# Keeping the rotated queries and keys of retention heads 1 to 3 as two fp32r parts, and loading the parts as operands

## The chip, the core and the metric

The kernel runs on one core of one Trainium2 chip. The metric is the device time of one execution in microseconds (us), shown as the median of several runs. The engines are TensorE (PE, with its weight loads as PEld), VectorE (DVE), ScalarE (ACT), GpSimd (POOL) and SyncE (SP), whose queue issues nearly all DMA transfers.

## What is computed

A trunk of two layers on a sequence of 1024 tokens of width 1024, all in float32. Layer 0 mixes tokens by forgetting attention, layer 1 by retention; each mixer is followed by a SwiGLU feed-forward block of width 2816, all with RMS norms and residuals. The part that matters here is the retention mixer:

```python
q = rotate(q, cos, sin)                 # 4 heads, 256 wide each
k = rotate(k, cos, sin) * (dk ** -0.5)
def rotate(t, cos, sin):
    t1, t2 = t[..., :half], t[..., half:]
    return concatenate([t1 * cos - t2 * sin, t1 * sin + t2 * cos])
# per head, in chunks of 64, with decay:
a = (q @ k.T) * d_intra
inner, cross = a @ v, (q @ state) * q_decay
state = state * chunk_decay + (k * k_decay).T @ v
y = inner + cross    # then normalised over the 512 columns of a head, gated, projected
```

## The kernel before, in words

Activations lie transposed: 128 features on the partitions, 1024 tokens along the row, in two halves of 512 (`HALF`). TensorE multiplies in fp32r. To keep float32 accuracy each operand is held as two fp32r parts, `hi` (the value cast to fp32r) and `lo` (what the cast left over). `split` (L97 to L99) makes them: ScalarE casts (L98), VectorE subtracts (L99). A product of two split operands is three matmuls (hi hi, hi lo, lo hi). The projections use a fast matrix scheme with seven products instead of eight for a 2x2 block of blocks (`Products`, L634 to L676); each product is 4 x 3 matmuls of 512 columns (L653 to L655), and ScalarE copies a sum from one PSUM bank to another or to SBUF between them (L662, L686, L689).

The retention layer has two stages.

*Projections.* `in_turn` (L678) walks over the weight blocks of keys, gates and queries of the four heads, two per head of gates and one each of keys and queries, and hands each result, four 128x512 blocks c11 to c22, to `projected` (L1000). For keys and queries `rotated` (L960 to L971) does the rotation in two halves: four products by cosine and sine on VectorE (L964 to L967), one subtraction and one addition on GpSimd (L968, L969), and two stores of 256 KB through SP into DRAM tiles `qd` or `kd` (L970, L971). In between, `values` (L973) projects the values of each head with `pair_N` (matmuls L771 to L773 of 256 columns) and stores them in `vd`.

*Heads.* `prepare` (L1090) loads a head. `load_k` (L1045) brings the two 128x1024 key tiles of a head into staging tiles `st` (L1050, 512 KB each), splits them into eight operand tiles `b` of pool `bpa` (L1051, through `bsplit` and L98, L99), transposes the same staged data with TensorE (L1060), and scales and splits the transposes (L1065, L1066). `load_units` (L801, called on L1092) loads the two query tiles into `st` (L805) and splits them into eight operand tiles of `bpa`. `load_v` (L1036) loads eight 256 KB blocks of values into `st` (L1038), takes off the mean and splits them into pool `bpb` (L1041 on ScalarE, L1042 on VectorE). Then `scores` (L1105 to L1107, evicted on L1116 and L1121), `weighted` (L1131 to L1133), `crossed` (L1142 to L1144), `state` (L1080 to L1082) and `finish` (L1146) follow for each of the eight pairs of head and half. `prepare(h + 1)` stands in the program at the second half of head h.

Three sets of buffers matter. The staging tag `st` has five tiles of 128x1024 and serves keys, queries, values and weights. `bpa` has 32 operand tiles of 128x512; a head takes 24 of them (8 keys, 4 transposed keys, 8 queries, 4 state). The pool `yp` has 16 tiles tagged `y`, from which `rotated` takes its intermediates.

No order is written out by hand around the change. The program is traced by a framework (the context on L1300) that plans each engine's order of instructions on a timeline of its own before the kernel runs, and places the semaphores. On the chip every engine and the SP queue work strictly in that order, so an instruction that waits holds up everything behind it on its queue.

Of the kernel before, what the change touches and what calls it, by code (L numbers as in the profile page):

```python
# [10 lines left out]
F32 = mybir.dt.float32  # L11
F32R = mybir.dt.float32r
# [5 lines left out]
P = 128  # L18
S = 1024
D = 1024  # L20
KT = D // P
H = 512
# [3 lines left out]
RET_HEADS = 4  # L26
# [11 lines left out]
def trunk(ctx, tc, nc, d, out):  # L38
    cp = ctx.enter_context(tc.tile_pool(name="cp", bufs=1))
    yp = ctx.enter_context(tc.tile_pool(name="yp", bufs=16))  # L40
    dp = ctx.enter_context(tc.tile_pool(name="dp", bufs=1, space=DRAM))

    def const(name, shape):
        t = cp.tile(shape, F32, tag=name, name=name)
        nc.sync.dma_start(t, d[name])
        return t
# [8 lines left out]
    def nm(s):  # L55
        cnt[0] += 1
        return f"{s}_{cnt[0]}"
# [5 lines left out]
    bpa = ctx.enter_context(tc.tile_pool(name="bpa", bufs=32))  # L63
# [4 lines left out]
    def mm_ps():  # L68
        tag, n = (("mm", 3), ("st", 2), ("pv", 2), ("mm", 3), ("st", 2), ("pv", 2), ("mm", 3))[banks[0] % 7]
        banks[0] += 1  # L70
        return mp.tile([P, H], F32, tag=tag, name=nm("mm"), bufs=n)

    def yu(s):
        return yp.tile([P, H], F32, tag="y", name=nm(s))

    def units(pool):
        return [pool.tile([P, H], F32R, tag="b", name=nm("b")) for _ in range(2)]
# [19 lines left out]
    def split(hi, lo, src):  # L97
        nc.scalar.copy(hi, src)  # L98
        return nc.vector.tensor_tensor(lo, src, hi.bitcast(F32), op=ALU.subtract)  # L99
# [10 lines left out]
    HALF = (slice(0, H), slice(H, S))  # L110
# [76 lines left out]
    with ExitStack() as fs:  # L187
# [6 lines left out]
        def half(tag, bufs=2):  # L194
            if tag in ("t", "x"):
                return yp.tile([P, H], F32, tag="y", name=nm(tag))
            return fp.tile([P, H], F32, tag=tag, name=nm(tag), bufs={"rec": 1}.get(tag, bufs))
# [4 lines left out]
        for kt in range(KT):  # L202
            xs = []
            for h in range(2):
                t = half("t", 9)
# [16 lines left out]
        def k_head(h):  # L222
            kh = fp.tile([P, S], F32R, tag="kh", name=nm("kh"))
            kl = fp.tile([P, S], F32R, tag="kl", name=nm("kl"))
            proj_head(2 * h + 1, lambda b, ps: split(kh[:, HALF[b]], kl[:, HALF[b]], ps))
            return kh, kl

        def q_head(h):
            qh = fp.tile([P, S], F32R, tag="qh", name=nm("qh"))
            ql = fp.tile([P, S], F32R, tag="ql", name=nm("ql"))  # L230

            def evac(b, ps):
                t = half("qf")
                nc.vector.tensor_tensor(t, ps, R[:, HALF[b]], op=ALU.mult)
                split(qh[:, HALF[b]], ql[:, HALF[b]], t)

            proj_head(2 * h, evac)
            return qh, ql
# [180 lines left out]
        ks, pss = [], {}  # L419
        for h in range(2):  # L420
            ks.append([fp.tile([P, S], F32R, tag=t, name=nm(t)) for t in ("kh", "kl")])
            for b in range(2):
                tag, n = (("mm", 3), ("mm", 3), ("st", 2), ("st", 2))[2 * h + b]
# [9 lines left out]
        ident = const("ident", [P, P])  # L433
# [12 lines left out]
        qq = q_head(0)  # L446
        for h in range(FOX_HEADS):
            if h > 0:
                kk, qq = k1 if h == 1 else k_head(h), q_head(h)
# [16 lines left out]
        part = {}  # L466
        for i, (n, b) in enumerate(TILES):
            if i < 3:
                mm_u(ops[n, b], wo[n][6:], last_o[:1], b, first=False, last=(i < EVAC))
            else:  # L470
                if n == len(wo):
                    wo.append(wtile(d["fox_o"][n][:, :7 * P], 7))
                tag, bufs = TAGS[i]
# [19 lines left out]
    def bsplit(pool, src):  # L493
        hi, lo = units(pool)
        split(hi, lo, src)
        return hi, lo
# [304 lines left out]
    def load_units(pool, src, gate=None):  # L801

        r = []
        st = sp.tile([P, 1024], F32, tag="st", name=nm("st"), bufs=5)
        nc.sync.dma_start(st, src)  # L805
        if gate is not None:
            gt = sp.tile([P, 1024], F32, tag="st", name=nm("st"), bufs=5)
            nc.sync.dma_start(gt, gate)
            nc.vector.tensor_tensor(st, st, gt, op=ALU.mult)  # L809
        for h in range(2):  # L810
            r.append(bsplit(pool, st[:, HALF[h]]))
        return r
# [102 lines left out]
    for n in range(KT):  # L915
# [3 lines left out]
        for b in range(2):  # L919
            if (n, b) in ops:  # L920
                ps = ops[n, b]
            elif n < NPART:
                ps = mp.tile([P, H], F32, tag=("pv", "st")[b], name=nm("mm"), bufs=2)
            else:
                ps = mm_ps()
# [20 lines left out]
    X, nrm, nw = ffn(0, X, norm, xd, xd2, False, nw, MAP1)  # L946


    qd = [[dp.tile([P, S], F32, tag=f"qd{k}", name=f"qd{k}") for k in range(2 * h, 2 * h + 2)] for h in range(RET_HEADS)]
    kd = [[dp.tile([P, S], F32, tag=f"kd{k}", name=f"kd{k}") for k in range(2 * h, 2 * h + 2)] for h in range(RET_HEADS)]  # L950
    vd = [dp.tile([P, 2 * D], F32, tag=f"vd{k}", name=f"vd{k}") for k in range(TB)]
    gd = [dp.tile([P, S], F32, tag=f"gd{k}", name=f"gd{k}") for k in range(16)]
    zd = [dp.tile([P, S], F32, tag=f"zd{k}", name=f"zd{k}") for k in range(16)]
# [3 lines left out]
        nc.sync.dma_start(cos[h], d["ret_cos"][:, HALF[h]])  # L957
        nc.sync.dma_start(sin[h], d["ret_sin"][:, HALF[h]])

    def rotated(dst, c11, c12, c21, c22):  # L960
        for h, (t1, t2) in enumerate(((c11, c21), (c12, c22))):
            m1, m2, m3 = yu("m1"), yu("m2"), yu("m3")
            m4 = t2 if h else yu("m4")
            nc.vector.tensor_tensor(m1, t1, cos[h], op=ALU.mult)  # L964
            nc.vector.tensor_tensor(m2, t1, sin[h], op=ALU.mult)
            nc.vector.tensor_tensor(m3, t2, sin[h], op=ALU.mult)
            nc.vector.tensor_tensor(m4, t2, cos[h], op=ALU.mult)  # L967
            nc.gpsimd.tensor_tensor(m1, m1, m3, op=ALU.subtract)  # L968
            nc.gpsimd.tensor_tensor(m2, m2, m4, op=ALU.add)  # L969
            nc.sync.dma_start(dst[0][:, HALF[h]], m1)  # L970
            nc.sync.dma_start(dst[1][:, HALF[h]], m2)  # L971

    def values(h):  # L973
        cc = pair_N((d["ret_v"][2 * h], d["ret_v"][2 * h + 1]), X)
# [15 lines left out]
    def gates(p, c11, c12, c21, c22):  # L990
        if p == 0:
            rcs.append(rms(nrm, mp, "ms"))
        for k, h, c in ((0, 0, c11), (0, 1, c12), (1, 0, c21), (1, 1, c22)):
            o = c if h else yu("o")
            nc.vector.tensor_tensor(o, c, R[:, HALF[h]], op=ALU.mult)
            nc.scalar.activation(o, o, AF.Silu)
            nc.sync.dma_start(gd[2 * p + k][:, HALF[h]], o)

    rcs, vmean = [], {}
    def projected(i, *cc):  # L1000
        if i % 4 == 0:
            rotated(kd[i // 4], *cc)
        elif i % 4 == 2:
            rotated(qd[i // 4], *cc)
        else:
            gates(i // 2, *cc)

# [7 lines left out]
    for h in range(RET_HEADS):  # L1015
        srcs = todo[done:4 * h + 3]
        in_turn(srcs, X, lambda i, *cc: projected(done + i, *cc))
        done = 4 * h + 3
        values(h)
    in_turn(todo[done:], X, lambda i, *cc: projected(done + i, *cc))  # L1020

    rc = rcs[0]
# [13 lines left out]
    def load_v(h, b):  # L1036
        st = sp.tile([P, 1024], F32, tag="st", name=nm("st"), bufs=5)[:, :512]
        nc.sync.dma_start(st, vd[b][:, h * 512:(h + 1) * 512])  # L1038
        m = vmean[h][:, b:b + 1]
        hi, lo = units(bpb)  # L1040
        nc.scalar.activation(hi, st, AF.Identity, bias=m)  # L1041
        nc.vector.scalar_tensor_tensor(lo, st, m, hi.bitcast(F32), op0=ALU.add, op1=ALU.subtract)  # L1042
        return hi, lo

    def load_k(h):  # L1045

        ks, kf = [], []
        for e in range(2):
            st = sp.tile([P, 1024], F32, tag="st", name=nm("st"), bufs=5)
            nc.sync.dma_start(st, kd[h][e])  # L1050
            ks.append([bsplit(bpa, st[:, HALF[i]]) for i in range(2)])  # L1051
            kf.append(st)
        kt = []
        for i in range(2):
            ps = mm_ps()
            for b in range(2):
                for e in range(2):
                    tk = slice((2 * i + b) * P, (2 * i + b + 1) * P)
                    c = (2 * b + e) * P
                    nc.tensor.transpose(ps[:, c:c + P], kf[e][:, tk], ident)  # L1060
            hi, lo = units(bpa)
            for b in range(2):
                r = kap[:, h, 2 * i + b:2 * i + b + 1]
                c = slice(b * 256, (b + 1) * 256)
                nc.scalar.activation(hi[:, c], ps[:, c], AF.Copy, scale=r)  # L1065
                nc.vector.scalar_tensor_tensor(lo[:, c], ps[:, c], r, hi[:, c].bitcast(F32),  # L1066
                                               op0=ALU.mult, op1=ALU.subtract)
            kt += [(hi[:, b * 256:(b + 1) * 256], lo[:, b * 256:(b + 1) * 256]) for b in range(2)]
        return ks, kt
# [19 lines left out]

    def prepare(h):  # L1090
        kk, kt = load_k(h)
        qq = [load_units(bpa, qd[h][e]) for e in range(2)]  # L1092
        vv = [load_v(h, b) for b in range(TB)]
        heads[h] = [kk, kt, qq, vv, None, []]

# [50 lines left out]
    def finish(h, ib, yps):  # L1146
# [21 lines left out]
        for vt in range(4):  # L1168
# [5 lines left out]
            nc.sync.dma_start(zd[4 * h + vt][:, HALF[ib]], ys[vt])  # L1174

    prepare(0)
    heads[0][4] = state(heads[0][1], heads[0][3])
    stages = [(h, ib) for h in range(RET_HEADS) for ib in range(2)]
# [21 lines left out]
    for n in range(KT):  # L1200
        w = wtile2(d["ret_o"][n], 8)
        for h in range(2):
            ps = mm_ps()
# [101 lines left out]
```

## Time and profile before

| what | value |
|---|---|
| median of 3 runs | 2585.12 us (2584.18 to 2586.54) |
| profiled execution, own time | 2588.21 us |
| span of its instructions | 2586.4 us |
| granted clock of TensorE over the span | 0.998 |
| moved by DMA over the span | 312.12 MB, mean 121 GB/s |
| projections of the retention layer | about 1140 to 1585 us |
| heads of the retention layer | about 1585 to 1745 us |

The span runs from the first to the last instruction; the profiled execution's own time is 1.8 us longer. A matmul's busy time overlaps the next one's, because matmuls are pipelined, so an engine's busy share is read together with its waits and with the spacing of its instructions. Waits are inferred from semaphores: "A <- B" means that A's engine stood idle and that B ended the wait. Transfers are timed from their issue on the queue to their landing.

### The profile page before, as it was taken

What the parts mean: (1) busy time and instruction counts of PE and PEld (TensorE: products, weight loads), DVE (VectorE), ACT (ScalarE), POOL (GpSimd) and SP (SyncE); (2) the same over time, 40 slices, a digit from 0 to 9 for tenths busy, and PEclk for the clock granted to TensorE, in tenths of its full rate; (3) what the DMA queues carried; (4) which work ended last, traced back from release to release, by engine and by line L of the source; (5) the groups of instructions that cost most, each with busy time, mean ns of one, the idle gap of its engine ahead of it and who ended that gap; (6) DMA issues with size and microseconds to landing.
All of it is one profiled execution on the core that took longest, in us unless ns stands there. A gap on an engine that the chain in (4) does not pass through costs nothing.

```text
span 2586.4 us, 35236 instructions
## 1 busy us (share of the span) xinstructions
PE 2561.6 (99%) x12812; PEld 2183.4 (84%) x12812; DVE 1837.3 (71%) x3130; ACT 1230.9 (48%) x2322; POOL 203.0 (8%) x203
## 2 busy tenths in 40 slices
PE   9999999999999999999999999999999999999998
PEld 8889887888888887889898989898888888888888
DVE  6798888866666767886656576785567666667794
ACT  6566666543333455454343435662354333335543
POOL 0143323000000001001000010000000000000200
PEclk9999999999999999999999999999999999999999
DMA  3111142422332344533232325555522333325541
GB/s 132 44 58 62 54 147 91 154 103 97 114 106 94 124 161 151 185 112 115 102 118 99 110 98 168 187 187 191 204 98 82 110 98 106 103 89 188 168 149 66
DMA packets 138286, 312.12 MB, mean 121 GB/s; under 512 B 16128, under 2 KB 29440, under 8 KB 138112
## 3 DMA queue, kind: packets, MB, share of 16 engines
q1 hardware_dynamic: 132912, 294.65, 33.8%
q0 software_dynamic: 4480, 14.68, 1.7%
q8 instruction: 100, 1.64, 0.3%
q14 instruction: 74, 0.61, 0.1%
q10 hardware_dynamic: 720, 0.55, 0.1%
HBM read 217.54 MB, written 92.27 MB: 120 GB/s over the span
## 4 chain that ended last, share of the span: by engine, by line
PE 92%; DVE 2%; issue 2%; DMA 2%; ACT 1%; POOL 0%; SPq 0%; POOLq 0%; DVEq 0%; ACTq 0%
PE mm L654 18%; PE mm L653 18%; PE mm L655 18%; PE mm L106 7%; PE mm L107 7%; PE mm L108 7%; PE mm L773 2%; PE mm L771 2%; PE mm L772 2%; DMA st<-vd 1%; PE mm L260 1%; PE mm L259 1%; PE mm L258 1%; PE rw L167 1%; PE pv L365 1%
## 5 line engine op out<-in xcount | busy, mean ns | idle before, releaser
L654 PE MATMUL mm<-b,wh 128*128 128x512 f32 x2128 | 827.9, 389 | 1.2 <-DVE b L99 1.2
L653 PE MATMUL mm<-b,wh 128*128 128x512 f32 x2128 | 825.5, 390 | 2.4 <-ACT u L686 1.2
L655 PE MATMUL mm<-b,wl 128*128 128x512 f32 x2128 | 824.4, 389 | 0.0
L98 ACT CAST wh<-st 128x512 fp32r<-128x512 f32 (+4 forms) x450 | 277.2, 617 | 527.5 <-PE mm L654 323.3
L653 PEld LDWEIGHTS mm<-b,wh 128*128 128x128 f32 x2128 | 399.6, 188 | 85.8 <-ACT u L686 1.7
L654 PEld LDWEIGHTS mm<-b,wh 128*128 128x128 f32 x2128 | 399.6, 188 | 83.5 <-DVE b L99 1.6
L655 PEld LDWEIGHTS mm<-b,wl 128*128 128x128 f32 x2128 | 399.5, 188 | 82.8
L99 DVE TENSOR_TENSOR wl<-st,wh 128x512 fp32r<-128x512 f32 (+4 forms) x450 | 318.9, 712 | 190.8 <-ACT wh L98 185.4
L98 ACT CAST wh<-s 128x512 fp32r<-128x512 f32 x252 | 156.9, 624 | 318.0 <-PE mm L654 282.7
L106 PE MATMUL mm<-b,wh 128*128 128x512 f32 x736 | 286.0, 392 | 7.2 <-ACT b L126 5.0
L107 PE MATMUL mm<-b,wh 128*128 128x512 f32 x736 | 287.6, 391 | 1.7 <-DVE b L99 1.7
L108 PE MATMUL mm<-b,wl 128*128 128x512 f32 x736 | 287.2, 391 | 0.0
L99 DVE TENSOR_TENSOR wl<-s,wh 128x512 fp32r<-128x512 f32 x252 | 180.5, 718 | 97.3 <-ACT wh L98 93.2
L106 PEld LDWEIGHTS mm<-b,wh 128*128 128x128 f32 x736 | 138.7, 188 | 36.6 <-ACT b L126 5.4
L107 PEld LDWEIGHTS mm<-b,wh 128*128 128x128 f32 x736 | 138.8, 189 | 29.5 <-DVE b L99 2.2
L108 PEld LDWEIGHTS mm<-b,wl 128*128 128x128 f32 x736 | 138.8, 189 | 28.3
L772 PE MATMUL mm<-wl,b 128*128 128x256 f32 x448 | 126.6, 283 | 0.0
L771 PE MATMUL mm<-wh,b 128*128 128x256 f32 x448 | 126.2, 283 | 0.0
L773 PE MATMUL mm<-wh,b 128*128 128x256 f32 x448 | 126.2, 283 | 0.0
L501 POOL DMA_DIRECT2D b<-ac_B x24 | 13.5, 561 | 1403.8 <-PE mm L654 1400.3
L98 ACT CAST b<-st 128x512 fp32r<-128x512 f32 (+1 forms) x160 | 92.2, 610 | 56.6 <-DVE st L809 18.2
L99 DVE TENSOR_TENSOR b<-st,b 128x512 fp32r<-128x512 f32 (+1 forms) x160 | 103.7, 678 | 13.5 <-ACT b L98 13.3
(507 smaller groups left out, 4047.1 us busy)
## 6 DMA issues: line engine op xcount, KB each, us to landing
st<-ffn_in SPq DMA_DIRECT2D x88, 512.0 KB, 3.5
st<-ffn_out_pairs SPq DMA_DIRECT2D x32, 512.0 KB, 4.0
ac_T<-t SPq DMA_DIRECT2D x48, 256.0 KB, 2.4
xo<-xd SPq DMA_DIRECT2D x32, 256.0 KB, 2.9
ac_B<-t SPq DMA_DIRECT2D x32, 256.0 KB, 2.4
st<-ac_T SPq DMA_DIRECT2D x16, 512.0 KB, 4.8
b<-ac_T POOLq DMA_DIRECT2D x32, 256.0 KB, 5.3
st<-ret_qk SPq DMA_DIRECT2D x16, 512.0 KB, 4.5
```

What stands on the lines that cost most here:

```text
L98: nc.scalar.copy(hi, src)
L99: return nc.vector.tensor_tensor(lo, src, hi.bitcast(F32), op=ALU.subtract)
L106: nc.tensor.matmul(ps, wh, xh, start=(first and k == 0), stop=False, skip_group_check=free)
L107: nc.tensor.matmul(ps, wh, xl, start=False, stop=False, skip_group_check=free)
L108: nc.tensor.matmul(ps, wl, xh, start=False, stop=(last and k == n - 1), skip_group_check=free)
L167: nc.tensor.matmul(ps[:, b * P:(b + 1) * P], col[:, b:b + 1].to_broadcast([P, P]), ident, start=True, stop=True)
L653: nc.tensor.matmul(ps, hi[:, js], th, start=first and j == 0, stop=False, skip_group_check=True)
L654: nc.tensor.matmul(ps, hi[:, js], tl, start=False, stop=False, skip_group_check=True)
L655: nc.tensor.matmul(ps, lo[:, js], th, start=False, stop=(j == 3), skip_group_check=True)
L771: nc.tensor.matmul(o, th[:, tk], hi[:, js], start=f, stop=False, skip_group_check=True)
L772: nc.tensor.matmul(o, th[:, tk], lo[:, js], start=False, stop=False, skip_group_check=True)
L773: nc.tensor.matmul(o, tl[:, tk], hi[:, js], start=False, stop=(j == 3), skip_group_check=True)
```

## The change

In heads 1 to 3, `rotated` now splits each rotated tile where it is made and stores both parts, in DRAM tiles of their own; for keys the first half is stored unsplit as well (`kf`), since `load_k` transposes it. The splits use tiles m3 or m4 for the `hi` part and the tile itself (or, for that first half of keys, one more `y` tile `ml`) for the `lo` part. When a head is prepared, the new `load_parts` loads the parts straight into `bpa` operand tiles, sixteen transfers of 256 KB for keys and queries, and the unsplit first half of the keys (two transfers of 256 KB) goes into staging tiles for the transposes. Head 0 keeps the old way. Loads go through the same SP queue.

```diff
--- before.py
+++ after.py
@@ -946,8 +946,14 @@
     X, nrm, nw = ffn(0, X, norm, xd, xd2, False, nw, MAP1)
 
 
-    qd = [[dp.tile([P, S], F32, tag=f"qd{k}", name=f"qd{k}") for k in range(2 * h, 2 * h + 2)] for h in range(RET_HEADS)]
-    kd = [[dp.tile([P, S], F32, tag=f"kd{k}", name=f"kd{k}") for k in range(2 * h, 2 * h + 2)] for h in range(RET_HEADS)]
+
+
+    def kept(s):
+        return dp.tile([P, S], F32, tag=s, name=s)
+
+    qd = [[kept(f"qd0{e}") if h == 0 else [kept(f"qd{h}{e}{s}") for s in "hl"] for e in range(2)] for h in range(RET_HEADS)]
+    kd = [[kept(f"kd0{e}") if h == 0 else [kept(f"kd{h}{e}{s}") for s in "hl"] for e in range(2)] for h in range(RET_HEADS)]
+    kf = [[dp.tile([P, H], F32, tag=f"kf{h}{e}", name=f"kf{h}{e}") for e in range(2)] for h in range(1, RET_HEADS)]
     vd = [dp.tile([P, 2 * D], F32, tag=f"vd{k}", name=f"vd{k}") for k in range(TB)]
     gd = [dp.tile([P, S], F32, tag=f"gd{k}", name=f"gd{k}") for k in range(16)]
     zd = [dp.tile([P, S], F32, tag=f"zd{k}", name=f"zd{k}") for k in range(16)]
@@ -957,7 +963,7 @@
         nc.sync.dma_start(cos[h], d["ret_cos"][:, HALF[h]])
         nc.sync.dma_start(sin[h], d["ret_sin"][:, HALF[h]])
 
-    def rotated(dst, c11, c12, c21, c22):
+    def rotated(dst, plain, c11, c12, c21, c22):
         for h, (t1, t2) in enumerate(((c11, c21), (c12, c22))):
             m1, m2, m3 = yu("m1"), yu("m2"), yu("m3")
             m4 = t2 if h else yu("m4")
@@ -967,8 +973,17 @@
             nc.vector.tensor_tensor(m4, t2, cos[h], op=ALU.mult)
             nc.gpsimd.tensor_tensor(m1, m1, m3, op=ALU.subtract)
             nc.gpsimd.tensor_tensor(m2, m2, m4, op=ALU.add)
-            nc.sync.dma_start(dst[0][:, HALF[h]], m1)
-            nc.sync.dma_start(dst[1][:, HALF[h]], m2)
+            for e, (m, hi) in enumerate(((m1, m3), (m2, m4))):
+                if not isinstance(dst[e], list):
+                    nc.sync.dma_start(dst[e][:, HALF[h]], m)
+                    continue
+                lo = m
+                if plain and h == 0:
+                    nc.sync.dma_start(plain[e], m)
+                    lo = yu("ml")
+                split(hi.bitcast(F32R), lo.bitcast(F32R), m)
+                for part, t in zip(dst[e], (hi, lo)):
+                    nc.sync.dma_start(part[:, HALF[h]], t)
 
     def values(h):
         cc = pair_N((d["ret_v"][2 * h], d["ret_v"][2 * h + 1]), X)
@@ -999,9 +1014,9 @@
     rcs, vmean = [], {}
     def projected(i, *cc):
         if i % 4 == 0:
-            rotated(kd[i // 4], *cc)
+            rotated(kd[i // 4], kf[i // 4 - 1] if i else None, *cc)
         elif i % 4 == 2:
-            rotated(qd[i // 4], *cc)
+            rotated(qd[i // 4], None, *cc)
         else:
             gates(i // 2, *cc)
 
@@ -1042,14 +1057,28 @@
         nc.vector.scalar_tensor_tensor(lo, st, m, hi.bitcast(F32), op0=ALU.add, op1=ALU.subtract)
         return hi, lo
 
+    def load_parts(src):
+
+        r = [[None, None], [None, None]]
+        for i in range(2):
+            for e in range(2):
+                r[e][i] = units(bpa)
+                for t, part in zip(r[e][i], src[e]):
+                    nc.sync.dma_start(t.bitcast(F32), part[:, HALF[i]])
+        return r
+
     def load_k(h):
 
-        ks, kf = [], []
+        ks = load_parts(kd[h]) if h else []
+        ts = []
         for e in range(2):
             st = sp.tile([P, 1024], F32, tag="st", name=nm("st"), bufs=5)
+            ts.append(st)
+            if h:
+                nc.sync.dma_start(st[:, :H], kf[h - 1][e])
+                continue
             nc.sync.dma_start(st, kd[h][e])
             ks.append([bsplit(bpa, st[:, HALF[i]]) for i in range(2)])
-            kf.append(st)
         kt = []
         for i in range(2):
             ps = mm_ps()
@@ -1057,7 +1086,7 @@
                 for e in range(2):
                     tk = slice((2 * i + b) * P, (2 * i + b + 1) * P)
                     c = (2 * b + e) * P
-                    nc.tensor.transpose(ps[:, c:c + P], kf[e][:, tk], ident)
+                    nc.tensor.transpose(ps[:, c:c + P], ts[e][:, tk], ident)
             hi, lo = units(bpa)
             for b in range(2):
                 r = kap[:, h, 2 * i + b:2 * i + b + 1]
@@ -1089,7 +1118,7 @@
 
     def prepare(h):
         kk, kt = load_k(h)
-        qq = [load_units(bpa, qd[h][e]) for e in range(2)]
+        qq = load_parts(qd[h]) if h else [load_units(bpa, qd[h][e]) for e in range(2)]
         vv = [load_v(h, b) for b in range(TB)]
         heads[h] = [kk, kt, qq, vv, None, []]
 
```

## Rows read from the trace of the kernel before

**Rows 1.** The page's head and section 1: busy us (share) and instructions.

```profile
span 2586.4 us, 35236 instructions
...
PE 2561.6 (99%) x12812; PEld 2183.4 (84%) x12812; DVE 1837.3 (71%) x3130; ACT 1230.9 (48%) x2322; POOL 203.0 (8%) x203
```

**Rows 2.** Waits of PE, projections and heads: us in total, times, longest.

```profile
PE mm L1060 <- DVE wl L1121: 1.6, 1, 1.6
PE mm L1132 <- DVE wl L1121: 0.3, 1, 0.3
```

**Rows 3.** Busy time by windows: PE, PEld, DVE, ACT, POOL, clock, DMA share, GB/s.

```profile
1140.00:1585.00 445.00, 445.00 (x2607) 396.26 (x2606) 283.15 (x426) 179.82 (x394) 50.29 (x32) 1.00 0.33 110
1585.00:1745.00 160.00, 158.05 (x911) 141.54 (x910) 128.15 (x298) 106.21 (x231) 0.00 (x0) 1.00 0.57 185
```

**Rows 4.** The chain of waits, 1646 to 1664 us: start us, us, what.

```profile
1647.30 7.67 DMA st<-vd
...
1656.53 2.95 DMA st<-vd
...
1661.43 0.27 DVE wl L1121
...
1661.84 0.63 PE mm L1060 x4
1662.46 0.23 PE mm L1142
```

**Rows 5.** Waits of ACT, 1585 to 1745 us: us in total, times, longest.

```profile
ACT b L1041 <- DMA st<-vd: 20.5, 13, 4.8
```

**Rows 6.** The SP queue in order of time, 1632 to 1676 us: start, us.

```profile
1633.12 1.56 SPq L1050 DMA_DIRECT2D st<-kd  x2
1635.02 1.05 SPq L805 DMA_DIRECT2D st<-qd  x2
1636.67 0.32 SPq L1038 DMA_DIRECT2D st<-vd  x1
...
1647.30 0.38 SPq L1038 DMA_DIRECT2D st<-vd  x1
...
1656.53 9.39 SPq L1038 DMA_DIRECT2D st<-vd  x5
```

**Rows 7.** ACT in order of time, 1663 to 1673 us: start us, us.

```profile
1670.16 1.15 ACT L98 CAST b<-st 128x512 fp32r<-128x512 f32 x2
```

**Rows 8.** Groups by line, 1585 to 1745 us: busy us, mean ns, idle before.

```profile
L98 ACT CAST b<-st 128x512 fp32r<-128x512 f32 x41 | 24.0, 619 | 1.1 <-DVE st L809 1.0
...
L99 DVE TENSOR_TENSOR b<-st,b 128x512 fp32r<-128x512 f32 x40 | 26.6, 689 | 0.3 <-ACT b L98 0.3
```

**Rows 9.** Groups by line, 1140 to 1585 us: busy us, mean ns, idle before.

```profile
L99 DVE TENSOR_TENSOR wl<-st,wh 128x512 fp32r<-128x512 f32 x91 | 71.9, 796 | 31.2 <-ACT wh L98 30.8
L968 POOL TENSOR_TENSOR m<-m,m 128x512 f32<-128x512 f32 x16 | 23.6, 1476 | 501.4 <-DVE m L966 257.9 <-DMA st<-ret_v 163.4 <-ACT wh L98 69.1
L967 DVE TENSOR_TENSOR u<-u,cos 128x512 f32<-128x512 f32 x8 | 9.8, 1230 | 0.0
L969 POOL TENSOR_TENSOR m<-m,m 128x512 f32<-128x512 f32 x8 | 13.9, 1744 | 0.0
```

**Rows 10.** DMA queues and issues, 1585 to 1745 us; issues with us to landing.

```profile
q1 hardware_dynamic: 12751, 29.49, 56.2%
...
st<-vd SPq DMA_DIRECT2D x31, 256.0 KB, 3.5
```

**Rows 11.** Source line L413: ns min/median/max, first and last start us.

```profile
L413 SPq DMA_DIRECT2D b<-od0h x2: 320/622/923, 358.7 to 360.1; - x2
...
DMA to landing us min/median/max: 3.4/5.3/7.1
```

**Rows 12.** Source line L970: the stores of rotated tiles, ns min/median/max.

```profile
L970 SPq DMA_DIRECT2D qd<-m x8: 320/320/382, 1195.0 to 1551.7; - x8
```

## The prediction, made before the changed kernel was run

> **What bounds the kernel now.** I read the page first, then the waits, then the windows of the two stages that the change touches, then the chain of waits at the one place where those stages lose time. TensorE is busy for 2561.6 of 2586.4 us [rows 1]; what another engine saves is worth something only where TensorE stood idle. In the projections it did not: 445 of 445 us busy, with VectorE at 283 and ScalarE at 180 us, so both have room [rows 3]. In the heads it was busy for 158 of 160 us, and its waits there are two, 1.6 us before a transpose and 0.3 us before L1132 [rows 2, 3]. That 1.9 us is nearly all that the change can give back.
>
> Where the 1.6 us comes from is seen in the chain. A value load issued at 1647.30 takes 7.67 us to land, the next is issued only at 1656.53 and takes 2.95 us, then the late VectorE work on L1121 releases the transpose at 1661.84 [rows 4]. ScalarE meanwhile waits at the head of its own queue for values: 20.5 us in 13 waits over the stage, the longest 4.8 us [rows 5]. The SP queue tells why the loads come singly. Two key tiles go into staging at 1633, two query tiles at 1635, one value block at 1636.67; that is all five `st` tiles. The next value blocks leave at 1647.30 and 1656.53 [rows 6]. The query tiles stay in staging until their splits, whose last two casts run at 1670.16 [rows 7], because the operand tiles are free no earlier; the keys stay until the transposes, 1661.84 [rows 4]. So for some 20 us the values share one staging tile.
>
> **The change, part by part.** *Splits.* Heads 1 to 3 have 8 splits each for keys and queries, 24 in all. Each leaves the heads stage with 0.62 us of ScalarE and 0.69 us of VectorE [rows 8], 14.9 and 16.5 us together. In the projections ScalarE's cost stays 14.9 us. For VectorE the same subtraction, 128x512, averages 0.80 us there [rows 9], so I take 24 x 0.80 = 19.1 us. VectorE goes from 283 to about 302, ScalarE from 180 to 195 of 445 us. I cost this at nothing, because TensorE covers it; without that cover it would cost at most the sum on the slower engine, 19 us.
>
> The reason why it is 0.80 and not 0.69 is in the rows: GpSimd works in that stage, 32 times, and in the heads never [rows 3], and the rotation's last product, which runs beside a GpSimd operation, takes 1.23 us [rows 9]. The Trainium skill's page GPSIMD Engine Reference, section Specifications, says that GpSimd's SBUF interfaces are shared with VectorE, with contention against VectorE instructions with two SBUF inputs. That rule speaks against moving subtractions next to the rotation: were every one of them slowed to 1.23 us, VectorE would pay 29.5 us and not 19.1. The cover would still hold, and the sum would be the same.
>
> *Stores.* A rotated query tile pair makes 8 stores for 4, keys 10 for 4: 3 x (4 + 6) = 30 more of 256 KB. An issue takes 0.32 us [rows 12], so 9.6 us of the SP queue over 400 us, in a stage where DMA is at a share of 0.33 [rows 3]. Nothing on the path. They come about 1.5 to 3 us later than before, behind a cast and a subtraction, and the weight loads queued behind them on SP come later by as much. Without the weights' head start that would be on the path up to 12 times; no TensorE wait in this stage says that the head start is short [rows 2, 3]. Cost nothing, at worst 3 us at each of a few places.
>
> *Loads.* Per head 4 loads of 512 KB become 16 parts and 2 unsplit halves of 256 KB: 2.10 MB become 4.72, and 14 more issues of 0.32 us, 4.5 us of SP. Over three heads that is 7.9 MB more. SP's hardware queue took 56.2% of 160 us for 29.49 MB [rows 10], 3.05 us per MB; 7.9 MB add 24 us of DMA time, a share of about 71%. It fits on average. In a burst it does not vanish: a head's load grows from 6.4 to 14.4 us of DMA time, and the values and the stores of results issued behind it wait for it.
>
> *Staging.* Only the two unsplit key tiles hold `st` now; two of five instead of four. Three value blocks can be under way together where one could. This takes away what made the 1.6 us. Gain: 1.9 us with the small one, at least 0 if the burst delays the values by as much, at most these 1.9 us.
>
> *Where the new wait goes.* Before, the data lay in staging when an operand tile came free, and a split made it ready in 0.62 + 0.69 = 1.3 us. Now the transfer itself starts when the tile is free, and TensorE waits for the landing, with all its later matmuls behind it. Behind the same wait on SP stand the values, the gates and the result stores. The trace has no such load in this stage. The nearest is on L413, where a burst of 24 parts of 256 KB was loaded straight into tiles of the same pool: 3.4, 5.3 and 7.1 us to landing at least, in the middle and at most [rows 11]. So an operand is ready 2.1 to 5.8 us later after its tile's release than with the split. What TensorE feels of it is bounded below by 0, since none of its waits names a transfer [rows 2], and above by 6 groups of loads (keys and queries of three heads) times the longest wait that a late load has caused on any engine here, 4.8 us [rows 5], 29 us. I take 0, nearest to the row of L413, whose parts nothing waited for, and because the planner puts other matmuls between load and use; the upper end goes into the range.
>
> **The sum.** -1.9 us for staging, 0 for the rest. Against the profiled execution, 2588.2 us with a span of 2586.4 [rows 1], that is 2586.3; the profiled execution lies 3.1 us above the median of the runs, so against the median of 2585.1 the forecast is 2583.2 us. A measurement of this kernel can tell about 0.2%, 5.2 us, from no change, so this counts as no change. The forecast's own range is 2581.5 to 2587, from one small wait more or less on either side.
>
> **Rivals.** *Slower: TensorE waits for the parts.* Its order was planned on expected landings. Where a landing is later than planned, ScalarE has taken the delay so far: on average 20.5 / 13 = 1.6 us a wait [rows 5]. If the delay moves to TensorE at each of the 6 groups, 9.5 us come and 1.9 go: 2592.7. It decides wherever the first use follows the tile's release by less than the landing, 3.4 to 7.1 us. For it: after the query casts at 1670.16 nothing is held back in staging any more, and the burst takes 14.4 us. Against it: the key tiles are asked for some 28 us before the transposes that use them (1633 to 1661) [rows 4, 6], so only the queries are tight. Chance 0.18.
>
> *Slower: ScalarE stands behind GpSimd.* In the projections a cast now waits for a rotation on GpSimd, 1.48 and 1.74 us for the two halves of a pair [rows 9], and holds up PSUM copies behind it. A copy has the cover of one product, 12 matmuls of 0.23 us [rows 4], 2.8 us, less a cast of 0.62: 2.1 us. One GpSimd operation is covered; both in a row, 3.2 us, are short by 1.1 us. With 12 halves, 13 us come and 1.9 go: 2596. Chance 0.07, since ScalarE idles for 265 of 445 us [rows 3].
>
> *Faster: TensorE's busy share hides room.* In the heads the weight loads are busy for 141.5 of 160 us [rows 3]; were the other 18.5 us lost to slow operands, their relief by 15 us of ScalarE work could give up to that: 2566.6. Against it: matmuls follow each other at 0.23 us right behind the wait that I found [rows 4], and no wait but two is shown. The page Perfetto Trace Analysis of the Trainium skill, section Identifying the Most-Contended Engine, has the rule that matmul busy time is a bad measure and the share of weight loads a good one; by that rule there is 16% of headroom over the span. By the waits there is 1.9 us. Chance 0.03.
>
> *The change does not bring its relief.* The planner may use the freed staging tiles for other loads, so that the values still come singly: 2585.1 and no change. Chance 0.05; the forecast keeps 0.67.
>
> **Numbers.** No change: the forecast 0.67, the missing relief 0.05, and of the first rival 0.02 where it strikes once or twice: 0.74. Slower: 0.16 and 0.07, 0.23. Faster: 0.03. The range runs from 2581.5, the low end of the forecast, to 2593, the whole of the first rival, and leaves out the other two.
>
> **What would show it.** Right: no wait of TensorE on L1060; ScalarE's waits on values well under 20.5 us; DMA share in the heads near 0.7; TensorE still busy for 445 of 445 us in the projections. Wrong: TensorE waiting for transfers into `b` in the heads, or for ScalarE in the projections while ScalarE waits for GpSimd; or a heads stage shorter by more than 2 us.

## The result, and the profile of the changed kernel

The changed kernel takes 2588.85 us (median of 22 runs, 2585.61 to 2590.65) against 2585.08 us (22 runs, 2583.38 to 2586.64): ratio 1.0014, interval 1.0008 to 1.0019, or 3.8 us more. A second set of runs gave 2587.35 against 2584.65 us: ratio 1.0010, interval 1.0002 to 1.0019. The kernel is slower, by less than the 0.2% that the prediction took for the edge of what can be told, and clear of the interval with this many runs. The prediction, 2583.2 us and no change, had the sign wrong. The measured time lies above 2587, the forecast's own upper end. Inside the whole range, 2581.5 to 2593, it lies by luck: the upper end was there for a wait of TensorE for the parts, and the changed kernel has no such wait.

The profiled execution hides this. Its own time, 2588.59 us, is a normal one, but that of the kernel before, 2588.21, lies 3.1 us above its median, so the two profiles nearly agree. What differs has to be read from the stages. The windows of the two stages, as in [rows 3]:

```profile
1140.00:1585.00 445.00, 445.00 (x2610) 396.29 (x2609) 288.15 (x448) 192.63 (x418) 58.90 (x32) 1.00 0.37 128
1585.00:1745.00 160.00, 157.37 (x897) 139.98 (x896) 113.70 (x271) 93.81 (x205) 0.00 (x0) 0.99 0.70 233
```

The projections took the splits, the stores and the additional waits of ScalarE without any idle time of TensorE. In the heads VectorE has 14 and ScalarE 12 us less to do, the DMA share is 0.70 as forecast, and TensorE is still busy for less of the stage than before. The mean granted clock of the heads is 0.99 and not 1.00. TensorE's waits in the heads (columns as in [rows 2]):

```profile
PE mm L1160 <- ACT wh L1149: 1.9, 1, 1.9
PE mm L1161 <- DVE wl L1150: 0.4, 1, 0.4
PE mm L1109 <- DVE wl L1150: 0.2, 1, 0.2
```

And ScalarE's waits on values, against [rows 5]:

```profile
ACT b L1056 <- DMA st<-vd: 12.9, 5, 4.4
```

So all four signs that the prediction named for being right are there: no wait on the transposes (L1060, now L1089), 12.9 us of ScalarE's waits on values instead of 20.5, a DMA share of 0.70, and TensorE busy for 445 of 445 us in the projections. The kernel is slower all the same.

The wait before a transpose is gone. In its place stands one at L1160, which was L1131: the first matmul of `weighted` for head 0. It waits for ScalarE, and ScalarE's own order shows what for (start, duration; L1056 was L1041, the cast of a value block, and the casts into `wh` are the scores of head 0 that TensorE waits for):

```profile
1607.54 0.72 ACT L1056 ACTIVATE b<-st,vmean 128x512 fp32r<-128x512 f32 x1 [3.22 <-DMA st<-vd]
...
1608.63 0.73 ACT L1056 ACTIVATE b<-st,vmean 128x512 fp32r<-128x512 f32 x1
...
1610.22 0.71 ACT L1056 ACTIVATE b<-st,vmean 128x512 fp32r<-128x512 f32 x1
1610.83 0.28 ACT L98 CAST wh<-atd 128x128 fp32r<-128x128 f32 x1
```

Head 0's eight value blocks are cast by then. These three belong to head 1, whose values TensorE first needs at 1643.40 (`state`, L1109), some 36 us later, and they stand in ScalarE's queue ahead of the scores that TensorE needs at once. The first waits 3.22 us for a load issued at 1602.91 that took 4.54 us to land; the scores wait behind it. On VectorE's queue, too, the second half of the first of these blocks (L1057 at 1608.29) stands ahead of all four scores.

The loads of head 1's values left SP earlier than before. The kernel before (its second profile, see below), where two query tiles take staging first and the first value block goes alone (columns as in [rows 6]):

```profile
1602.53 1.75 SPq L805 DMA_DIRECT2D st<-qd  x2
1604.84 0.38 SPq L1038 DMA_DIRECT2D st<-vd  x1
...
1613.22 9.24 SPq L1038 DMA_DIRECT2D st<-vd  x3
```

The changed kernel, which issues a third block at 1605.24:

```profile
1602.91 1.75 SPq L1053 DMA_DIRECT2D st<-vd  x2
```

What comes after the wait is as large as the wait. TensorE in order of time:

```profile
1609.34 0.39 PE L1136 MATMUL mm<-b,b 128*128 128x512 f32 x1
1611.64 1.35 PE L1160 MATMUL mm<-wh,b 128*128 128x512 f32 x3 [1.92 <-ACT wh L1149]
1613.39 0.80 PE L1161 MATMUL mm<-wl,b 128*128 128x512 f32 x1 [0.40 <-DVE wl L1150]
1613.98 0.63 PE L1162 MATMUL mm<-wh,b 128*128 128x512 f32 x1
1614.41 0.63 PE L1161 MATMUL mm<-wl,b 128*128 128x512 f32 x1
1614.83 0.63 PE L1162 MATMUL mm<-wh,b 128*128 128x512 f32 x1
1615.26 0.47 PE L1161 MATMUL mm<-wl,b 128*128 128x512 f32 x1
1615.57 0.39 PE L1162 MATMUL mm<-wh,b 128*128 128x512 f32 x1
1615.80 0.51 PE L1160 MATMUL mm<-wh,b 128*128 128x384 f32 x2
```

Matmuls of 512 columns that follow each other at 0.23 us elsewhere [rows 4] start 0.43 us apart here. From 1609.34 to 1615.80 ten such matmuls start, 2.3 us of work in 6.5 us: 4.2 us lost, of which 2.3 us are the two waits. The rest, 1.9 us, goes with the granted clock, which is at the lower of its two levels, 1.2 GHz, for most of the stretch from 1612 to 1616 us (the column before the last two):

```profile
1612.00:1616.00 4.00, 3.60 (x11) 2.43 (x10) 3.59 (x12) 1.76 (x7) 0.00 (x0) 0.57 0.83 229
```

### The profile page after: what moved, and what is told of

Read it like the earlier page. It is cut to its first block, busy times and chain, and to the rows that moved or that the text cites. A ratio compares the mean times of both kernels' runs of the same rounds, so it can differ in the third digit from the quotient of the medians.

```text
span 2586.8 us, 35404 instructions
## 1 busy us (share of the span) xinstructions
PE 2562.7 (99%) x12812; PEld 2182.9 (84%) x12812; DVE 1829.4 (71%) x3130; ACT 1230.7 (48%) x2322; POOL 210.2 (8%) x203
## 4 chain that ended last, share of the span: by engine, by line
PE 92%; DMA 2%; DVE 2%; ACT 2%; issue 1%; SPq 0%; POOL 0%; DVEq 0%; POOLq 0%; ACTq 0%
PE mm L654 18%; PE mm L653 18%; PE mm L655 18%; PE mm L106 7%; PE mm L107 7%; PE mm L108 7%; PE mm L773 2%; PE mm L771 2%; PE mm L772 2%; PE mm L260 1%; PE mm L259 1%; PE mm L258 1%; PE mm L1161 1%; PE mm L1162 1%; PE mm L1160 1%
## 5 line engine op out<-in xcount | busy, mean ns | idle before, releaser
L99 DVE TENSOR_TENSOR wl<-st,wh 128x512 fp32r<-128x512 f32 (+4 forms) x450 | 309.9, 693 | 190.7 <-ACT wh L98 187.1
L99 DVE TENSOR_TENSOR wl<-s,wh 128x512 fp32r<-128x512 f32 x252 | 179.8, 715 | 91.8 <-ACT wh L98 87.5
L605 DVE TENSOR_TENSOR s<-st 128x512 f32<-128x512 f32 x84 | 58.2, 693 | 65.6 <-DMA st<-ffn_in 28.9
L98 ACT CAST b<-st 128x512 fp32r<-128x512 f32 (+1 forms) x136 | 77.6, 606 | 54.4 <-DVE st L809 18.3
```

Source lines behind the costliest of these rows:

```text
L605: nc.vector.tensor_tensor(self.s1, self.a21, self.a22, op=ALU.add)
```

## The experiments

Two theories stood at the start. **A, one place:** freed staging tiles let head 1's value loads start earlier, and the planner put their casts ahead of head 0's first scores; a late landing then holds ScalarE, and TensorE with it. **B, traffic:** 7.9 MB more in the heads stage make many loads late. Each kernel below was timed in turn with the kernel before on one chip.

### The changed kernel again

No edit.

> The changed kernel once more, for a second profile and for times beside the experiments. Theory A (one place): TensorE waits some 2 us for head 0's first weighted matmuls behind ScalarE, which waits for a value block of head 1; whether the granted clock falls to 1.2 GHz there differs from run to run. Expected about 2588.8 us and this wait again. Theory B (traffic): the loss of 3.8 us is spread over many small waits of the heads stage, from 7.9 MB more to move; expected about 2588.8 us with several waits of different places.

Measured: 2587.35 us, ratio 1.0010 (1.0002 to 1.0019). The profile has the same wait, 1.9 us on L1160 behind ScalarE, and the same fall of the clock from 1611 to 1615 us; TensorE's only other wait in the stage is 0.2 us. One place, twice, is A's reading. The time came out 1.5 us below the expected 2588.8.

### ScalarE's order alone

```diff
     def load_v(h, b):
...
-        nc.scalar.activation(hi, st, AF.Identity, bias=m)
+        with tc.issue_after(first_scores[0]) if h == 1 else nullcontext():
+            nc.scalar.activation(hi, st, AF.Identity, bias=m)
```

`first_scores[0]` is the last of ScalarE's casts in head 0's first four scores.

> The changed kernel, with ScalarE's casts of head 1's values placed behind the casts of head 0's first scores on ScalarE's queue; nothing else. Theory A: TensorE's wait of 1.9 us on the first weighted matmul goes, and with it the fall of the clock behind it; 2584 to 2585.5 us, level with the kernel before. Theory B: the traffic is the same, so the time stays at 2588 to 2589 us.

Measured: 2585.49 us, ratio to the kernel before 1.0007 (0.9998 to 1.0016), 1.9 us below the changed kernel in the same set of runs, though the two intervals overlap. The wait on L1160 and the low clock behind it are gone. All of TensorE's waits in the stage are now one:

```profile
PE mm L1137 <- DMA b<-qd10h: 1.7, 1, 1.7
```

L1137 is the first matmul of `scores`. That is the prediction's first rival: TensorE waits for the landing of a query part. The chain of waits runs through it (SPq is SP issuing, here two value blocks and four gate blocks; start and duration):

```profile
1625.98 0.32 SPq L1053
1626.35 0.43 SPq L1053
...
1628.24 0.43 SPq L1207
1628.72 6.96 DMA b<-qd10h
...
1635.81 0.76 PE mm L1137 x3
```

The part is issued behind six loads and takes 7 us to land. In this run the wait came as soon as the other was gone.

### Queries alone, keys alone

```diff
-    kd = [[kept(f"kd0{e}") if h == 0 else [kept(f"kd{h}{e}{s}") for s in "hl"] for e in range(2)] for h in range(RET_HEADS)]
+    kd = [[kept(f"kd{h}{e}") if h >= 0 else [kept(f"kd{h}{e}{s}") for s in "hl"] for e in range(2)] for h in range(RET_HEADS)]
...
-        ks = load_parts(kd[h]) if h else []
+        ks = []
...
-            if h:
-                nc.sync.dma_start(st[:, :H], kf[h - 1][e])
-                continue
```

This is queries alone (`h >= 0` holds for every head, so keys are stored as before); keys alone is the same edit on `qd` and `qq`.

> Only the queries are kept as parts; keys as in the kernel before. Theory A: the queries' staging tiles are the ones that come free for value blocks, so the early value cast and the wait come with this half alone; 2588 to 2589 us. Theory B: 3.1 of the 7.9 MB are added, so 40% of the 3.8 us; about 2586.6 us.

> Only the keys are kept as parts; queries as in the kernel before. Theory A: four of five staging tiles stay taken by keys and queries, values still come singly, so no wait at the first weighted matmul; 2584.5 to 2585.5 us. Theory B: 4.7 of the 7.9 MB are added, so 60% of the 3.8 us; about 2587.4 us.

Measured: queries alone 2589.41 us, ratio 1.0017 (1.0008 to 1.0026); keys alone 2586.57 us, ratio 1.0008 (0.9999 to 1.0017). TensorE's waits in the heads, queries alone:

```profile
PE mm L1157 <- ACT wh L1146: 2.5, 1, 2.5
```

and keys alone:

```profile
PE mm L1109 <- DVE rs_d L153: 1.2, 1, 1.2
PE mm L1089 <- DVE yv L1191: 1.1, 1, 1.1
```

Half of the change, with less than half of the added traffic, costs no less than the whole (the intervals overlap), and at the same place (L1157 is `weighted` there). On ScalarE's queue two casts of head 1's values stand ahead of the first scores with queries alone, three with the whole change, none with keys alone and none in the kernel before. (With keys alone one stands ahead of the fourth score, and no wait of TensorE comes of it.) So the step is the one from staged queries to unstaged ones, as A has it. Keys alone missed A's number by 1.1 us and B's by 0.8: two waits of another kind, behind small VectorE operations, took 2.3 us in its profile. Whether the keys' traffic has a part in them was not separated.

### Queries alone, with ScalarE's order

The edit of ScalarE's order on queries alone.

> Queries alone as parts, with head 1's value casts behind the casts of head 0's first scores. Theory A: the wait of 2.5 us at the first weighted matmul and the fall of the clock behind it go, 4 us or more off the 2589.4 us of queries alone; 2584 to 2585.5 us, unless the queries' landing is waited for as in the run with both, which would leave 2586. Theory B: no change of traffic, so 2589 us.

Measured: 2586.08 us, ratio 1.0004 (0.9995 to 1.0012), 3.3 us below queries alone, though in another set of runs. The wait at the first weighted matmul fell to 0.3 us; the landing of the query parts is waited for again:

```profile
PE mm L1134 <- DMA b<-qd10h: 1.5, 1, 1.5
PE mm L1164 <- DVE wl L1153: 0.3, 1, 0.3
```

### Both orders

To ScalarE's order a second one is added: head 1's value blocks 3 to 7 are issued on SP behind its query parts.

```diff
-        nc.sync.dma_start(st, vd[b][:, h * 512:(h + 1) * 512])
+        with tc.issue_after(parts_in[-1]) if h == 1 and b > 2 else nullcontext():
+            nc.sync.dma_start(st, vd[b][:, h * 512:(h + 1) * 512])
```

> The changed kernel with the casts in the better order, and head 1's value blocks 3 to 7 queued on SP behind head 1's query parts. If TensorE's wait of 1.7 us for the landing of head 1's queries comes from the value blocks and gate blocks ahead of them on SP, it goes, and the stage has no wait left: 2582.5 to 2584 us, below both kernels. If it comes from the transfers' own length under the added traffic, it stays: 2585.5 us or more, or comes back for the values.

> The version with both orders changed once more: 2584.1 us the first time, 0.9 us below the kernel before, less than the interval. With theory A its stage has no wait of TensorE over 0.5 us, and 2583.5 to 2584.5 us come again, 1 to 1.9 us below the kernel before.

Measured: 2584.08 us, ratio 0.9996 (0.9987 to 1.0005), and 2584.49 us, ratio 0.9994 (0.9986 to 1.0003). TensorE has no wait in the heads in either profile, and in the second its window reads:

```profile
1585.00:1745.00 160.00, 160.00 (x925) 143.71 (x924) 116.96 (x276) 94.81 (x209) 0.00 (x0) 1.00 0.69 235
```

The traffic is that of the changed kernel, at a share of 0.69 against 0.70, and the loss is gone: with these two orders the traffic of the change costs nothing that can be told. This version is below the changed kernel, and 0.9 to 1.1 us below the kernel before, which neither interval tells from nothing.

### The order of the loads without ScalarE's

From the version with both orders ScalarE's is taken out again:

```diff
-        with tc.issue_after(first_scores[0]) if h == 1 else nullcontext():
-            nc.scalar.activation(hi, st, AF.Identity, bias=m)
+        nc.scalar.activation(hi, st, AF.Identity, bias=m)
```

> The changed kernel with head 1's value blocks 3 to 7 queued on SP behind its query parts, but ScalarE's queue left as planned: three of head 1's value casts still stand ahead of the casts of head 0's first scores. Theory A: the wait of about 2 us at the first weighted matmul stays, 2587 to 2588.5 us. If the order of the loads alone was the cause, it goes, 2584 us.

Measured: 2589.66 us, ratio 1.0013 (1.0004 to 1.0022). This is 5.2 us above the version with both orders in the same set of runs, and the intervals of the two to the kernel before do not touch (1.0004 to 1.0022 and 0.9986 to 1.0003). The two kernels differ in ScalarE's order alone, so this pair shows best that this order is the cause. A's range, up to 2588.5, was passed by 1.2 us. The wait is back, and larger:

```profile
PE mm L1169 <- ACT wh L1158: 2.1, 1, 2.1
PE mm L1170 <- DVE wl L1159: 0.8, 1, 0.8
```

### Traffic alone, in the kernel before

```diff
         qq = [load_units(bpa, qd[h][e]) for e in range(2)]
+        for i in range(5 if h else 0):
+            t = dp.tile([P, S], F32, tag=f"cp{h}{i}", name=f"cp{h}{i}")
+            for c in range(2):
+                with tc.issue_after(loads[0]):
+                    nc.sync.dma_start(t[:, HALF[c]], kd[h][i % 2][:, HALF[c]])
```

> The kernel before with 7.9 MB more to move in the heads stage: per head 1 to 3 ten copies of 256 KB from the keys to a place that nobody reads, issued behind the head's query loads. Theory A: traffic alone costs little; within 2 us of the kernel before, 2584 to 2586.5 us, with the order of ScalarE's queue at the first scores as before. Theory B: the traffic is the cause; 2588 us or more.

Measured: 2592.45 us, ratio 1.0028 (1.0018 to 1.0038), 7.5 us more. A's number was missed by 6 us and B's threshold is passed. (`loads[0]` is the load of a query tile; the copies stand behind it on SP.) TensorE's longer waits in the heads:

```profile
PE mm L1082 <- DVE wl L1128: 2.4, 1, 2.4
PE mm L1112 <- DVE rs_d L153: 1.9, 1, 1.9
```

ScalarE's wait on values in the same kernel (before: [rows 5]):

```profile
ACT b L1043 <- DMA st<-vd: 26.0, 14, 5.1
```

The copies stand on SP between the query loads and the values: head 1's first value block leaves at 1616.31, in the kernel before at 1606.77. The wait of 2.4 us, at a matmul of `state`, ends a chain that begins with a value load issued at 1631.19 and landing after 5.71 us. So traffic can cost more than the whole change, where it stands on SP just ahead of value loads that ScalarE waits for at the head of its queue. The two waits are not at the first weighted matmul. Why it does not come to that in the changed kernel is not shown; there three value blocks of head 1 leave ahead of all its parts. The copies also write what they read, which loads do not, so this is no exact copy of the change's traffic.

### Values without staging, in the kernel before

```diff
-        st = sp.tile([P, 1024], F32, tag="st", name=nm("st"), bufs=5)[:, :512]
+        hi, lo = units(bpb)
+        st = lo.bitcast(F32)
         nc.sync.dma_start(st, vd[b][:, h * 512:(h + 1) * 512])
         m = vmean[h][:, b:b + 1]
-        hi, lo = units(bpb)
```

> The kernel before with nothing of the change, but with values loaded straight into the tiles of their low parts and split there, so that they need no staging and never come singly. My forecast's step was that values sharing one staging tile make the 1.6 us wait before a transpose. If that step was right, this wait is gone; none of head 1's value casts stands ahead of head 0's first scores here in a late place, so no new wait there: 2582.5 to 2584.5 us. If the wait came from elsewhere, 2584.7 us as before.

Measured: 2589.72 us, ratio 1.0016 (1.0007 to 1.0025), 4.7 us more where 0.5 to 2.5 less was expected. Nothing of the change is in it, and the bytes are those of the kernel before. TensorE's longer wait in the heads:

```profile
PE mm L1142 <- DVE atd L1116: 2.5, 1, 2.5
```

ScalarE's on values:

```profile
ACT b L1041 <- DMA b<-vd: 24.9, 12, 7.0
```

The wait is at a matmul of `crossed`. The chain of waits leads back to a value (start and duration; L1042 is VectorE's second half of a value block):

```profile
1613.38 4.61 DMA b<-vd
1618.01 0.73 ACT b L1041
...
1622.57 0.66 DVE b L1042
1623.42 0.27 DVE atd L1116
1623.74 0.50 PE mm L1142
```

This is head 1's first value block. It lands after 4.61 us, ScalarE's casts and VectorE's halves of this and the next blocks follow, with two splits of staged tiles (L99), and the work on the score (L1116) that releases TensorE stands behind them in VectorE's queue. The loss is of the same kind as in the changed kernel: work on head 1 stands ahead of a score of head 0.

But the run does not test what it was meant to test. A value load no longer waits for staging; it needs a free pair of tiles of `bpb`, and the loads of this version leave later than before, not earlier. Head 0's eight blocks leave from 1583.17 to 1594 in the kernel before; here the first leaves at 1589.44 and the last two at

```profile
1607.62 0.88 SPq L1039 DMA_DIRECT2D b<-vd  x2
```

Head 1's first block leaves at 1613.38 and not at 1606.77. So the values were not given more room here, and that ScalarE waits 24.9 us and not 20.5 says nothing against the staging step. That step is tested by the changed kernel itself, where ScalarE's waits on values did fall, to 12.9 us.

### The kernel before again

No edit.

> The kernel before against itself, for the size of an accidental difference and a second profile of the heads stage. Expected 2585 us, ratio 1.000 within 0.0008, with the wait of about 1.6 us before a transpose again and no wait at the first weighted matmul.

Measured: 2586.06 us, ratio 1.0001 (0.9992 to 1.0009). The wait before a transpose is not in this profile. TensorE's only wait in the heads:

```profile
PE mm L1132 <- DVE wl L1121: 0.3, 1, 0.3
```

The window of the heads:

```profile
1585.00:1745.00 160.00, 159.69 (x920) 143.14 (x919) 131.18 (x302) 107.26 (x234) 0.00 (x0) 1.00 0.57 187
```

So the 1.6 us of [rows 2] stands in one of two profiles of the same kernel. The first was of an execution 3.1 us above its median, this one of an execution 2.9 us below; how often the wait comes in an execution at the median is not shown. The order of ScalarE around head 0's first scores in the kernel before, where the scores stand first and the value cast last:

```profile
1607.80 0.30 ACT L98 CAST wh<-atd 128x128 fp32r<-128x128 f32 x1
...
1610.19 0.31 ACT L98 CAST wh<-atd 128x128 fp32r<-128x128 f32 x1
1611.67 0.72 ACT L1041 ACTIVATE b<-st,vmean 128x512 fp32r<-128x512 f32 x1 [1.17 <-DMA st<-vd]
```

Here, too, the cast waits for its load, 1.17 us, and TensorE waits for nothing behind it. The load was issued at 1604.84 and took some 6.8 us to land, longer than the 4.54 us in the changed kernel: a late landing of head 1's first value block is nothing that the change brought, only its place in the order is.

## Why the prediction was wrong, step by step

**What bounds the kernel: right.** TensorE is busy for 445 of 445 us in the projections with the change as without, and the loss came from its waits in the heads and from the lower clock behind them.

**The splits, the stores: right.** Nothing of them reached TensorE. The 24 moved subtractions took 19.0 us, the 19.1 that I took, but not evenly: eighteen took 0.68 us each and six, beside the addition on GpSimd (L975), 1.12 us. These six are half of this group:

```profile
L99 DVE TENSOR_TENSOR m<-m,m 128x512 fp32r<-128x512 f32 x12 | 10.8, 898 | 11.0 <-ACT m L98 11.0
```

The prediction cited from the Trainium skill's page GPSIMD Engine Reference, section Specifications, that such VectorE instructions contend with GpSimd; the 1.12 against 0.68 us agree. As a worst case my 1.23 us was too low: in the kernel before, single subtractions of this stage took up to 1.78 us beside GpSimd and 0.69 us without. VectorE's total rose by 5 us only, from 283 to 288, and not to 302, mainly because other work beside GpSimd became shorter: the 91 subtractions of [rows 9] fell from 71.9 to 63.8 us.

**The second rival's mechanism came, its price did not.** ScalarE does stand behind GpSimd in the projections, and for longer than I had priced (L974 was L968):

```profile
ACT m L98 <- POOL m L974: 36.0, 12, 6.1
```

Three us a time on average, 6.1 us at most, and TensorE waited for none of it. What covers a PSUM copy is more than the 2.1 us that I took; how much more is not shown.

**The staging step is the one that failed: wrong in its size and in its sign.** It said that two of five tiles held instead of four "takes away what made the 1.6 us": gain 1.9 us, "at least 0". Its first half came true: ScalarE waited 12.9 us for values and not 20.5 (12.5 and 18.5 in the second profiles). What failed is what this is worth to TensorE. First, the 1.9 us were not there to gain in every execution: the second profile of the kernel before has only the 0.3. I had noted that the profiled execution lay 3.1 us above the median, and still counted its wait in full. Second, the lower bound of 0 left out where the casts of the freed values would stand. The three value blocks that "can be under way together" did start earlier, and this is what cost: the planned order has their casts ahead of scores that TensorE needs at once, and the first of them waited 3.22 us for its load. The new wait took 2.3 us and the lower clock behind it 1.9: 4.2 us, less some 0.3 us that the kernel before loses there too, near the 3.8 and 2.7 us measured in two sets. Placing these casts behind the scores removes it: 5.2 us lie between the two versions that differ in this order alone. That the planner moved the casts because their loads could leave earlier is read from the orders in the runs, three casts ahead with the whole change, two with queries alone, none with keys alone; the planner's own timeline is not on record.

**The direct wait for parts: held back, not absent.** In the changed kernel TensorE waits for no part, so the 0 that I took stands. The parts take about 5 to 6 us to land at the median, inside the 3.4 to 7.1 of [rows 11]. But with the cast order mended, TensorE waited 1.7 and 1.5 us for the landing of a query part; the mean price of 1.6 us a group was right, for one group of six. Putting the later value blocks behind the parts on SP took it away. I named both queues and looked for the wait at the parts, not at the values, whose place in the order the change moves as well.

**The third rival, hidden room, has no support.** With both orders TensorE is busy for 160.00 of 160 us and waits for nothing, and its weight loads are at 143.7 us, 90%. Removing every wait in this stage brought 0.9 to 1.1 us against the kernel before, which the intervals do not tell from nothing, with 12 us less of ScalarE's work. By the rule of the Trainium skill's page Perfetto Trace Analysis, section Identifying the Most-Contended Engine, a tenth of the stage would be headroom; no run here got any of it.

What stays open: how much of the 4.54 us that the load issued at 1602.91 took is due to the change's own traffic. The traffic is not needed for it: queries alone, with less of it, had a longer wait, and the kernel before, with none, a longer landing.

## What to carry to other kernels

A wait seen in one profile is worth only what it has in a second one: here 1.6 of the forecast 1.9 us stood in one of two profiles, that of an execution 3.1 us above the median. A sign can come true and be worth nothing: ScalarE waited 7.6 us less for values, and TensorE gained nothing by it. When a change frees buffers, ask which loads will be issued earlier and where their consumers then stand in a strictly ordered queue; an early cast of data that is needed late is a wait for whatever stands behind it. Such a loss is mended by ordering two instructions, not by giving the room back.

## What was not expected of the hardware

An idle time of TensorE of some 2 us can cost about that much again. In six profiles the longest wait of TensorE in the heads was 1.9 to 2.5 us (the changed kernel twice, queries alone, the loads' order alone, traffic alone, values without staging), and the granted clock fell to 1.2 GHz behind it each time. Behind a second wait of 1.92 us in the run with traffic alone, at 1724.44, it did not, nor behind the waits of 1.1 to 1.7 us in the heads. In the forgetting attention, around 393 us, all 13 profiles have the same wait of 1.7 us, and the clock falls behind it in six of them. The stretch from 395 to 400 us in the kernel before, then in the changed kernel (the clock is the column before the last two):

```profile
395.00:400.00 5.00, 5.00 (x18) 4.07 (x18) 2.93 (x6) 2.21 (x4) 2.38 (x3) 0.66 0.34 107
```

```profile
395.00:400.00 5.00, 4.73 (x22) 3.61 (x23) 4.01 (x9) 3.39 (x5) 2.59 (x4) 1.00 0.34 107
```

In 5 us 18 matmuls start instead of 22; four of 0.23 us are some 0.9 us. That can be part of why runs of one kernel differ by 3 to 5 us, and two single profiles are no comparison at this size.
